# The Strassen stage of a hybrid decoder block: right-hand sums by accumulating transfers, no GpSimd sums, gates kept on chip

## The chip, the cores and the metric

The kernel runs on one core of one Trainium2 chip. The metric is the device time of one execution in microseconds (us), lower is better; it is given as the median of several runs. Five engines matter: TensorE (PE in the profile; its weight loads are PEld), VectorE (DVE), ScalarE (ACT), GpSimd (POOL) and SyncE (SP), which here only issues transfers. ACT and POOL issue transfers too. Each engine works through its own list of instructions in order.

## The reference, cut to what matters

One layer, 1024 tokens plus 16 meta tokens, width 1024, all in float32:

```python
xn = rms_norm(x, norm_pre)
proj = xn @ w_in                       # columns of four kinds, split:
y_ssd = ssd_mixer(z, xbc, dt, ...)     # Mamba-2 style chunked scan, ends in an rms_norm
y_sc  = short_conv_mixer(b, c, h, g)   # b * conv3(c * h) * silu(g)
y_dn  = gated_deltanet_mixer(qkv, z, b, a, ...)
branch = [y_ssd @ w_branch[0], y_sc @ w_branch[1], y_dn @ w_branch[2]]
gates  = sigmoid(gate_logits)          # 3 x 1024 columns of proj
merged = sum_n gates[n] * branch[n]
out = x + rms_norm(merged @ w_out, norm_post)
```

Seven products of 1024 x 1024 x 1024 stand at the end: three gates (`xn` with the last columns of `w_in`), three branches (`y` with `w_branch`), and the output (`merged` with `w_out`).

## The kernel before

**Precision.** Every float32 product is made of three TensorE products of numbers split in two: `a = ah + al`, and `ah*bh + ah*bl + al*bh`. ACT makes the high part with a copy that rounds, DVE the low part with a subtraction.

**The dense stage**, about 1300 us. The normalised input stands in SBUF, transposed, as `xh` and `xl` (pool `xp`). 84 jobs (`jobs`, `run_jobs`, `dense`) each load 128 columns of `w_in`, split them (L144 ACT, L145 DVE) and multiply them with the whole stream. Beside them run the mixers: `dn_mix` for 8 heads, `sd_mix` for 8 pairs of heads, `sc_jobs` for 8 blocks of channels. `weave` puts the mixers' small steps between the dense matmuls: a mixer is a generator that yields the amount of dense work wanted before its next step, scaled by `GAPS[kind]`. Mixers use POOL for masks (`affine_select`, L474, L568), for clearing buffers (L621) and for two subtractions near their end (L699, L703). Their results go to DRAM: `y_dn`, `y_sc`, `y_sd`, one [128, 1024] tensor for each of 8 row blocks. The stream is stored to `x_d` after the norm: ACT issues a store of `xh`, and POOL an accumulating transfer that adds `xl` to it in DRAM (L942, L943), 8 of each. Scratch tiles of mixers come from one tag of 5 buffers (`tmp`).

**The Strassen stage**, from L961 on. Each of the seven large products (a group: `ORDER_C` = gates 2, 1, 0, branches 2, 1, 0, output) is done with Strassen's method in the Winograd form: the operands are cut into 2 x 2 blocks of 512 x 512, and 7 products of blocks (phases `ph` 0 to 6) replace 8. A phase is 48 matmuls of 128x128 by 128x512: 4 quarters `q` of 12. The left operand (weights for TensorE) has blocks `a11` to `a22`, the right one (moving) `b11` to `b22`. Phases need these sums:

- right: `b11-b12`, `t2 = b22-b11`, `b12-b22`, `b21-t2`: POOL, 8 instructions a group in `sums_after` (L1047, L1082) and `t_prep` (L1058);
- left: `s2 = a22-a21` on DVE (L1068), and `a11-a21`, `a11+s2`, `a12-s2` on POOL through `both` (L1047), 6 instructions a group; the output group makes its `a11-a21` on DVE.

`t_prep` splits the right operand of the next phase (`th` ACT L1034, `tl` DVE L1035, two halves), `w_prep` the left one (`wh` ACT L1041, `wl` DVE L1042). The three matmuls are L1101 (`wh`,`th`), L1102 (`wh`,`tl`) and L1103 (`wl`,`th`). Results gather in two pairs of PSUM banks, `y` and `z`; `take_copy` (L1110, ACT) copies `y` after phases 0, 2 and 3, and `finish` (L1149, DVE) adds the copy to `z` for three of the four blocks of the result. For a gate group `block_done` applies the sigmoid and stores it to DRAM (`gate_d`, L1122, L1123); for a branch group it loads the gate again (L1116), multiplies (L1131) and adds to `merged` (L1133). The output group ends in `out_piece`. Right-hand blocks of gates and of two branches are loaded by rows, four transfers of 256 KB a block (L982); weights by one of 1 MB (L987). `scale_tasks` (L1196 on) loads `y_sd`, scales it by the norm (L1212) and stores it as `ys_d`.

The pools of the dense stage are closed before the Strassen stage; its pools `c1` and `c2` lie in the space that is freed, so the first tiles wait for the last readers of what lay there (`c1`'s first blocks lie where `xh` and `xl` lay).

**What sets the order.** The source gives each instruction a priority by its place; a list scheduler with a cost model then writes each engine's list ahead of time: an instruction that is not ready in the plan lets a later one pass. On the chip the lists are fixed.

## Time and profile before

| | |
|---|---|
| median of 3 runs | 1930.35 us (1929.93 to 1933.7) |
| profiled execution, its own time | 1933.35 us |
| its span, first to last instruction | 1931.6 us |
| PE busy | 1835.5 us, 95% of the span |
| DVE busy | 1380.2 us, 71% |
| ACT busy | 825.7 us, 43% |
| POOL busy | 474.2 us, 25% |
| mean granted TensorE clock | 0.982 of full |

A busy PE is not PE at its peak, since ends of matmuls are modelled; idle time of an engine is put down to what released it. The span is cut below at 1300.1 us, where the last dense matmul ends, and then at the first matmul of each group, which is seen in the change of the PSUM bank that the matmuls write.

### The profile page before, as it was taken

To read this page: it belongs to the slowest core of one execution; us is meant where nothing else is said; L and a number is where in the kernel's file an instruction comes from. 1 tells how busy PE (TensorE), PEld (TensorE's weight loads), DVE (VectorE), ACT (ScalarE), POOL (GpSimd) and SP (SyncE) were. 2 spreads that over 40 slices of the span, in tenths; PEclk is the share of its full clock that TensorE was granted. 3 is DMA by queue.
4 is the path that set the end of the run, shared out by engine and by line. 5 is a ranking of instruction groups with operands and counts; after the bars stand their busy time and mean duration, and the time that the engine had idled before them with its cause. 6 is when DMAs were issued, how large, how long until landed. Compare 5 with 4: busy or idle time off the path is not lost.

```text
span 1931.6 us, 27668 instructions
## 1 busy us (share of the span) xinstructions
PE 1835.5 (95%) x11115; PEld 1580.9 (82%) x11115; DVE 1380.2 (71%) x1842; ACT 825.7 (43%) x1341; POOL 474.2 (25%) x393
## 2 busy tenths in 40 slices
PE   6999999999999999999999999995999999998977
PEld 5988988898889888888898898884777787786856
DVE  5565666657666656765667887865786788989997
ACT  5533434243342523444254554623535444343434
POOL 3101011010100101110011111107273563829340
PEclk9999999999999999999999999997999999999989
DMA  6711112111111111111222231217817355261602
GB/s 183 197 33 56 45 45 66 34 45 55 45 55 55 34 56 44 55 50 40 59 77 64 80 107 56 77 39 260 308 73 236 117 188 170 92 229 49 202 22 87
DMA packets 143658, 182.77 MB, mean 95 GB/s; under 512 B 10689, under 2 KB 96894, under 8 KB 142506
## 3 DMA queue, kind: packets, MB, share of 16 engines
q1 hardware_dynamic: 135898, 153.22, 25.0%
q10 hardware_dynamic: 6336, 23.07, 3.0%
q0 software_dynamic: 1296, 4.72, 1.2%
q8 instruction: 87, 1.43, 0.3%
q14 instruction: 41, 0.34, 0.1%
HBM read 138.93 MB, written 42.05 MB: 94 GB/s over the span
## 4 chain that ended last, share of the span: by engine, by line
PE 75%; DVE 12%; issue 5%; DMA 3%; POOL 3%; ACT 2%; SPq 0%; DVEq 0%; ACTq 0%; POOLq 0%
DVE tl L1035 3%; PE py L1103 3%; PE py L1102 3%; DVE wl L1042 3%; PE py L1101 3%; PE pz L1103 2%; PE pz L1102 2%; PE pz L1101 2%; POOL t L1058 1%; DMA a__13894<-in_w_in_dram 1%; DVE s L1068 1%; DMA b__13498<-x_d 0%; DVE U L1149 0%; POOL b__16016 L1047 0%; DMA gain<-in_norm_pre_dram 0%
## 5 line engine op out<-in xcount | busy, mean ns | idle before, releaser
L1101 PE MATMUL py<-th,wh 128*128 128x512 f32 x448 | 179.2, 400 | 23.9 <-ACT wh L1041 20.5
L1103 PE MATMUL py<-th,wl 128*128 128x512 f32 x448 | 179.6, 401 | 17.8 <-DVE wl L1042 17.7
L1102 PE MATMUL py<-tl,wh 128*128 128x512 f32 x448 | 179.7, 401 | 12.5 <-DVE tl L1035 12.5
L1103 PE MATMUL pz<-th,wl 128*128 128x512 f32 x336 | 133.0, 396 | 8.1 <-DVE wl L1042 8.1
L144 ACT CAST wh<-raw 128x1024 fp32r<-128x1024 f32 x84 | 88.0, 1048 | 117.7 <-DMA raw<-in_w_in_dram 7.5
L1102 PE MATMUL pz<-tl,wh 128*128 128x512 f32 x336 | 132.6, 395 | 2.1 <-DVE tl L1035 2.1
L1101 PE MATMUL pz<-th,wh 128*128 128x512 f32 x336 | 132.5, 394 | 0.0
L145 DVE TENSOR_TENSOR wl<-raw,wh 128x1024 fp32r<-128x1024 f32 x84 | 103.4, 1230 | 34.3 <-ACT wh L144 34.3
L1101 PEld LDWEIGHTS py<-th,wh 128*128 128x128 f32 x448 | 86.8, 194 | 43.5 <-ACT wh L1041 21.3
L1103 PEld LDWEIGHTS py<-th,wl 128*128 128x128 f32 x448 | 86.8, 194 | 40.1 <-DVE wl L1042 22.1
L1102 PEld LDWEIGHTS py<-tl,wh 128*128 128x128 f32 x448 | 86.9, 194 | 33.2 <-DVE tl L1035 15.1
L1103 PEld LDWEIGHTS pz<-th,wl 128*128 128x128 f32 x336 | 64.2, 191 | 23.2 <-DVE wl L1042 9.9
L1102 PEld LDWEIGHTS pz<-tl,wh 128*128 128x128 f32 x336 | 64.1, 191 | 16.5 <-DVE tl L1035 3.0
L1101 PEld LDWEIGHTS pz<-th,wh 128*128 128x128 f32 x336 | 64.1, 191 | 13.3
L1035 DVE TENSOR_TENSOR tl<-t,th 128x1024 fp32r<-128x1024 f32 x14 | 43.2, 3083 | 13.8 <-ACT th L1034 13.8
L1042 DVE TENSOR_TENSOR wl<-s,wh 128x1024 fp32r<-128x1024 f32 x14 | 39.6, 2836 | 0.0
L1149 DVE TENSOR_TENSOR U<-pz,U 128x1024 f32<-128x1024 f32 x26 | 31.6, 1217 | 10.3 <-PE pz L1103 10.3
L1110 ACT COPY U<-py 128x1024 f32<-128x1024 f32 x28 | 28.2, 1007 | 6.9 <-DVE ys L1212 5.4
L1122 ACT ACTIVATE U<-U 128x1024 f32<-128x1024 f32 x12 | 12.7, 1062 | 42.7 <-DVE U L1149 42.7
L455 ACT ACT_TABLE_LOAD x20 | 25.7, 1283 | 4.3 <-PE sd6z L168 1.0
L1041 ACT CAST wh<-s 128x1024 fp32r<-128x1024 f32 x14 | 14.7, 1051 | 26.3 <-DVE s L1068 23.7
L1034 ACT CAST th<-t 128x1024 fp32r<-128x1024 f32 x14 | 14.7, 1051 | 25.3 <-POOL t L1058 18.3
(1899 smaller groups left out, 6065.2 us busy)
## 6 DMA issues: line engine op xcount, KB each, us to landing
raw<-in_w_in_dram SPq DMA_DIRECT2D x84, 512.0 KB, 4.1
g<-gate SPq DMA_DIRECT2D x24, 512.0 KB, 3.7
gate<-U ACTq DMA_DIRECT2D x12, 512.0 KB, 4.9
x_d<-xh ACTq DMA_DIRECT2D x8, 512.0 KB, 6.8
x_d<-xl POOLq DMA_DIRECT2D x8, 512.0 KB, 10.1
ys<-y_sd SPq DMA_DIRECT2D x16, 256.0 KB, 6.1
ys_d<-ys ACTq DMA_DIRECT2D x4, 1024.0 KB, 8.3
xt<-in_x_dram SPq DMA_DIRECT2D x7, 512.0 KB, 4.7
```

What stands on the lines that cost most here:

```text
L144: A.copy(wh, raws[i])
L145: V.tensor_tensor(wl, raws[i], wh.bitcast(F32), ALU.subtract)
L455: lambda o, c0, n: A.activation(dst[:, c0 - META:c0 - META + n], o, fn), name=name)
L1035: V.tensor_tensor(l, src, h.bitcast(F32), ALU.subtract)
L1042: V.tensor_tensor(l, src, h.bitcast(F32), ALU.subtract)
L1058: GP.tensor_tensor(t2, tk(k["b22"], u), tk(k["b11"], u), SUB)
L1068: V.tensor_tensor(wk(g.s2, u), wk(k["a22"], u), wk(k["a21"], u), SUB)
L1101: PE.matmul(o, lhsT=wh[:, k, cs], rhs=r1, start=fresh and k == 0, stop=False, skip_group_check=not fresh)
L1102: PE.matmul(o, lhsT=wh[:, k, cs], rhs=r2, start=False, stop=False, skip_group_check=not fresh)
L1103: PE.matmul(o, lhsT=wl[:, k, cs], rhs=r1, start=False, stop=k == HK - 1, skip_group_check=not fresh)
L1110: A.copy(t, g.ps["y", u])
L1149: V.tensor_tensor(t, z, t, ADD)
```

## The change

- **Right-hand operands** are kept in DRAM as seven ready blocks of 1 MB for each of five streams `s` (x, dn, sc, sd, wo): `opd[s][o]`, with off-diagonal blocks stored negated (`n12`, `n21`). The four sums are made by `sums(s)`: POOL issues four copies DRAM to DRAM and four accumulating transfers, each of which needs the one before. No POOL arithmetic is left in the Strassen stage. Phases 1, 4 and 5 (`NEG`) negate the left operand while it is split.
- **Where the sums run**: `right_x` and `right_wo` step along with `dn_mix` of heads 0 and 2, `sums("dn")` with `sd_mix` 1, one step after every third yield (`beside`); `sums("sc")` follows the last sc job, `sums("sd")` the scale tasks. The stores of the stream after the norm are gone; `right_x` makes them.
- **Left-hand sums** are all on DVE (`left_sum`).
- **Loads**: each phase loads its right operand as two transfers of 512 KB, two phases ahead (`t_load`, 4 buffers). The first two phases read `xh` and `xl` in SBUF, whose pool moved to the right side of SBUF and closes after them.
- **Order**: groups are gate 2, branch 2, gate 1, branch 1, gate 0, branch 0, output. A gate stays in four SBUF tiles until the next group uses it; `gate_d` is gone.
- **Passing**: after phase 0 (not in the first group) ACT copies bank `y` into bank `z`, where phases 1 to 2 go on adding, so that block (0,0) needs no addition on DVE.
- The scale tasks run one at every quarter from phase 2 of the first group, not one at every second quarter in groups 1 and 2. `GAPS["sl"]` is 2.6, not 3.6.

```diff
-GAPS = {..., "sl": 3.6}
+GAPS = {..., "sl": 2.6}
-    xp, xp_st = hand_pool("xp")
+    xp, xp_st = hand_pool("xp", side="right")
...
+    OPS = ("11", "n21", "t2", "t3", "t1", "t4", "22")
+    opd = {s: {o: dram.tile([P, HK, HALF], F32, name=f"{s}_{o}") for o in OPS + ("n12",)}
+           for s in ("x", "dn", "sc", "sd", "wo")}
...
+    def sums(s):
+        o = opd[s]
+        for dst, a, b in (("t1", "n12", "11"), ("t2", "t1", "22"), ("t3", "n12", "22"), ("t4", "t2", "n21")):
+            GP.dma_start(o[dst], o[a])
+            yield 0
+            GP.dma_start(o[dst], o[b], accum_op=ALU.add, max_dma_last_dim=2048)
+            yield 0
...
-        DMA.dma_start(y_dn[h], zT)
+        for j in range(2):
+            DMA.dma_start(quarter("dn", h // HK, j)[:, h % HK, :], zT[:, j * HALF:(j + 1) * HALF])
...
-            DMA.dma_start(y_sc[t], acc)
+            if t == KT - 1:
+                for _ in sums("sc"):
+                    pass
...
+    def right_x():
+        o = opd["x"]
+        for i in range(2):
+            ks, ts = slice(i * HK, (i + 1) * HK), slice(META + i * HALF, META + (i + 1) * HALF)
+            dst = quarter("x", i, i)
+            A.dma_start(dst, xh[:, ks, ts].bitcast(F32))
+            GP.dma_start(dst, xl[:, ks, ts].bitcast(F32), accum_op=ALU.add)
+        yield 0
+        for i in range(2):
+            ts = slice(META + (1 - i) * HALF, META + (2 - i) * HALF)
+            for u in range(2):
+                ks = slice(i * HK + 2 * u, i * HK + 2 * u + 2)
+                dst = quarter("x", i, 1 - i)[:, 2 * u:2 * u + 2, :]
+                for part in (xh, xl):
+                    t = tmp(f"xn{i}{u}")[:, :SEQ].rearrange("p (k t) -> p k t", k=2)
+                    A.mul(t, part[:, ks, ts].bitcast(F32), -1.0)
+                    if part is xh:
+                        A.dma_start(dst, t)
+                    else:
+                        GP.dma_start(dst, t, accum_op=ALU.add)
+                    yield 0
+        yield from sums("x")
...
+    def beside(main, side, every=3):
+        side = side()
+        for n, want in enumerate(main()):
+            yield want
+            if n % every == 0:
+                next(side, None)
+        for _ in side:
+            pass
...
-    for k in range(KT):
-        A.dma_start(x_d[k], xh[:, k, META:].bitcast(F32))
-        GP.dma_start(x_d[k], xl[:, k, META:].bitcast(F32), accum_op=ALU.add)
...
+    def t_load(g, ph):
+        if from_stream(g, ph):
+            return
+        for u in range(2):
+            t = g.raw[ph, u] = c1.tile([P, 2, HALF], F32, name=f"tr{g.n}_{ph}{u}", tag="tr", bufs=4)
+            DMA.dma_start(t, g.ops[OPS[ph]][:, 2 * u:2 * u + 2, :])
...
+        if ph in NEG and not from_stream(g, ph):
+            A.mul(w[:, 0], src, -1.0)
+            V.scalar_tensor_tensor(w[:, 1], src, -1.0, w[:, 0].bitcast(F32), ALU.mult, SUB)
...
+    def left_sum(g, dst, x, y, op):
+        k = g.blk
+        for u in range(2):
+            V.tensor_tensor(wk(k[dst], u), wk(k[x], u), wk(k[y], u), op)
...
+        if ph == 0 and g.n:
+            g.ps["z", u] = bank("z")
+            A.copy(g.ps["z", u], g.ps["y", u])
+        elif ph in (0, 2, 3):
+            t = g.st[ph, u] = c1.tile([P, 2, HALF], F32, tag=f"u{ph or 3}", name=f"u{ph}_{g.n}{u}", bufs=2)
             A.copy(t, g.ps["y", u])
...
+            gt, m = gate[i, j][:, qs, :], quarter_tile(merged, "mg", i, j)[:, qs, :]
+            if g.b == ORDER[0]:
+                V.tensor_tensor(m, t, gt, ALU.mult)
+            else:
+                V.tensor_tensor(gt, t, gt, ALU.mult)
+                V.tensor_tensor(m, m, gt, ADD)
...
+            if q == 1:
+                if ph == 3:
+                    left_sum(g, "a11", "a11", "s2", ADD)
                 elif ph == 4:
+                    left_sum(g, "a12", "a12", "s2", SUB)
+                elif ph == 6 and nxt is not None and nxt.kind != "o":
+                    left_sum(nxt, "a21", "a11", "a21", SUB)
...
+            if (0, 2) <= (g.n, ph) and extra:
+                extra.pop(0)()
```

## Rows read from the trace of the kernel before

**Rows 1.** engines over stretches: dense stage, then gap, seven groups, tail; busy us (count)

```profile
core 0: us, PE busy (x) PEld busy (x) DVE busy (x) ACT busy (x) POOL busy (x), PEclk, DMA share, GB/s
0.00:1300.10 1300.10, 1279.41 (x8763) 1130.39 (x8763) 861.50 (x1481) 549.53 (x1037) 165.32 (x297) 1.00 0.22 64
1300.10:1311.80 11.70, 0.01 (x1) 0.00 (x0) 3.14 (x3) 3.15 (x4) 0.00 (x0) 0.72 0.90 307
1311.80:1415.10 103.30, 84.07 (x337) 66.96 (x338) 72.88 (x56) 43.96 (x45) 57.15 (x20) 0.88 0.70 260
1415.10:1494.90 79.80, 76.72 (x337) 62.89 (x336) 61.83 (x36) 40.46 (x42) 42.32 (x15) 1.00 0.45 152
1494.90:1576.20 81.30, 77.08 (x337) 62.83 (x336) 64.45 (x37) 41.38 (x43) 43.15 (x15) 1.00 0.50 169
1576.20:1656.90 80.70, 78.14 (x337) 63.96 (x336) 70.33 (x44) 35.70 (x36) 42.83 (x14) 0.98 0.48 162
1656.90:1740.80 83.90, 79.73 (x337) 64.76 (x336) 77.15 (x51) 34.24 (x34) 43.41 (x14) 0.96 0.42 145
1740.80:1828.00 87.20, 79.23 (x338) 64.08 (x337) 82.35 (x51) 34.02 (x35) 50.89 (x14) 0.96 0.42 139
1828.00:1920.00 92.00, 80.54 (x336) 64.97 (x335) 78.42 (x73) 40.92 (x63) 29.12 (x10) 0.93 0.10 35
1920.00:1931.60 11.60, 0.52 (x3) 0.09 (x1) 8.16 (x18) 2.33 (x7) 0.00 (x0) 0.63 0.49 181
```

**Rows 2.** TensorE, order of time: first and last of the final phase's 48 matmuls

```profile
1909.47 0.39 PE L1101 MATMUL pz<-th,wh 128*128 128x512 f32 x1
...
1920.13 0.39 PE L1103 MATMUL pz<-th,wl 128*128 128x512 f32 x1
```

**Rows 3.** TensorE's waits, Strassen stage: total us, times, longest

```profile
PE py L1101 <- ACT wh L1041: 20.5, 2, 11.7
PE py L1103 <- DVE wl L1042: 17.7, 6, 8.7
PE py L1102 <- DVE tl L1035: 12.5, 6, 3.5
```

**Rows 4.** order of time, VectorE, then GpSimd, in the second group: start, us

```profile
1433.19 3.41 DVE L1042 TENSOR_TENSOR wl<-s,wh 128x1024 fp32r<-128x1024 f32 x1
...
1432.13 3.38 POOL L1047 TENSOR_TENSOR a__13971<-a__13971,s 128x1024 f32<-128x1024 f32 x1
```

**Rows 5.** VectorE's groups (busy us, mean ns); a scalar_tensor_tensor of 1024 (min/median/max)

```profile
L1149 DVE TENSOR_TENSOR U<-pz,U 128x1024 f32<-128x1024 f32 x26 | 31.6, 1217 | 10.3 <-PE pz L1103 10.3
...
L1035 DVE TENSOR_TENSOR tl<-b__16016,th 128x1024 fp32r<-128x1024 f32 x4 | 4.9, 1217 | 0.0
...
L444 DVE SCALAR_TENSOR_TENSOR dn2q<-dn2qraw,cols,dn2q x3: 1277/1280/1281, 288.8 to 292.6; 128x1024 f32<-128x1024 f32 x3
```

**Rows 6.** order of time around the gap: SP's weight load, ACT's rounding of it

```profile
1303.20 0.51 SPq L987 DMA_DIRECT2D a__13473<-in_w_in_dram  x1
...
1310.74 1.99 ACT L1041 CAST wh<-a__13473 128x1024 fp32r<-128x1024 f32 x2 [1.80 <-DMA a__13473<-in_w_in_dram]
```

**Rows 7.** VectorE, first group: in-order wait for a load

```profile
  DMA a__13894<-in_w_in_dram: 8.9, 1
```

**Rows 8.** GpSimd's accumulating stores L943 in the dense stage: issue ns, landing

```profile
L943 POOL DMA_DIRECT2D x_d<-xl x8: 840/848/1046, 45.9 to 70.2; - x8
...
  DMA x_d<-xh: 22.1, 8
...
DMA to landing us min/median/max: 5.7/10.1/13.0
```

**Rows 9.** transfers by issue: KB each, median us to landing

```profile
ys_d<-ys ACTq DMA_DIRECT2D x4, 1024.0 KB, 8.3
```

**Rows 10.** GpSimd, order of time at the start and in a mixer

```profile
4.56 0.37 POOL L621 MEMSET dm0Z<- 16x8 f16 x2
...
131.37 0.56 POOL L621 MEMSET dm0Z<- 128x256 f16 x2 [5.16 <-PE dm0u L633]
```

More of the change, by code (lines that the diff above doesn't have):

```diff
@@ L126, in hybrid_block @@
     snw = pers.tile([P, KT], F32, name="snw")
+    nsnw = pers.tile([P, KT], F32, name="nsnw")
     xh = xp.tile([P, KT, TK], F32R, name="xh")
@@ L240, in hybrid_block @@
     eps2 = cst.tile([P, 1], F32, name="eps2")
+    ndnw = cst.tile([P, 1], F32, name="ndnw")
     def constants():
@@ L915, in hybrid_block @@
             lambda t=t, g=g: sd_mix(t, grps[g], sdt[t])]
+        mix = lambda gens=gens: chain(*gens)
+        if t == 1:
+            mix = lambda mix=mix: beside(mix, lambda: sums("dn"))
         fs = []
@@ L989, in cols_of, with __init__ @@
         return load
-    def kept(blocks):
-        def load(t, i, j):
-            DMA.dma_start(t, blocks[i, j])
-        return load
-    ORDER_C = [("g", b) for b in ORDER] + [("b", b) for b in ORDER] + [("o", 0)]
-    right = {0: kept(ys_d), 1: rows_of(y_sc), 2: rows_of(y_dn)}
-    merged = {}
-    class Group:
-        def __init__(self, n, kind, b):
-            self.n, self.kind, self.b = n, kind, b
-            self.blk, self.t, self.w = {}, {}, {}
-            if kind == "g":
-                self.wsrc, self.tsrc = cols_of(w_in, C_G + b * D), rows_of(x_d)
-            elif kind == "b":
-                self.wsrc, self.tsrc = cols_of(w_branch[b]), right[b]
-            else:
-                self.wsrc, self.tsrc = None, cols_of(w_out)
+    groups = []
+    merged, gate = {}, {}
+    class Group:
+        def __init__(self, kind, b):
+            self.n, self.kind, self.b = len(groups), kind, b
+            self.blk, self.raw, self.t, self.w, self.ps, self.st = {}, {}, {}, {}, {}, {}
+            self.wsrc = {"g": cols_of(w_in, C_G + b * D), "b": cols_of(w_branch[b])}.get(kind)
+            self.ops = opd["x" if kind == "g" else "wo" if kind == "o" else ("sd", "sc", "dn")[b]]
         def load(self, *tags):
@@ L1025, in tk, with from_stream @@
-    def tk(t, u):
-        return t[:, 2 * u:2 * u + 2, :]
+    for b in ORDER:
+        for kind in "gb":
+            groups.append(Group(kind, b))
+    groups.append(Group("o", 0))
+    last = len(groups) - 1
     def wk(t, u):
         return t[:, :, u * 256:(u + 1) * 256]
-    def t_split(g, ph, u, src):
+    NEG = (1, 4, 5)
+    BANK = "yzyyzyz"
+    LEFT = ("a11", "a12", "s2", "a21", "a11", "a22", "a12")
+    def from_stream(g, ph):
+        return g.n == 0 and ph < 2
+    def t_load(g, ph):
[4 more added lines that the diff above has]
+            DMA.dma_start(t, g.ops[OPS[ph]][:, 2 * u:2 * u + 2, :])
@@ L1112, in gates_in @@
-    def gates_in(g, i, j):
-        if g.kind == "b":
-            for u in range(2):
-                t = g.gt[i, j, u] = slab(f"g{g.n}_{i}{j}{u}")
-                DMA.dma_start(t, gate_d[g.b, i, j, u])
-    def block_done(g, i, j, u, t, in_psum):
+            PE.matmul(o, lhsT=w[:, 0, k, cs], rhs=r1, start=fresh and k == 0, stop=False, skip_group_check=not fresh)
+            PE.matmul(o, lhsT=w[:, 0, k, cs], rhs=r2, start=False, stop=False, skip_group_check=not fresh)
+            PE.matmul(o, lhsT=w[:, 1, k, cs], rhs=r1, start=False, stop=k == HK - 1, skip_group_check=not fresh)
@@ L1124, in block_done @@
         elif g.kind == "b":
-            gt = g.gt.pop((i, j, u))
-            first = g.b == ORDER[0]
-            if first and (i, j) not in merged:
-                merged[i, j] = c2.tile([P, HK, HALF], F32, name=f"mg{i}{j}", tag=f"mg{i}{j}")
-            m = merged[i, j][:, 2 * u:2 * u + 2, :]
-            s = m if first else gt if in_psum else t
-            V.tensor_tensor(s, t, gt, ALU.mult)
-            if not first:
-                V.tensor_tensor(m, m, s, ADD)
-        else:
-            out_quarter(g, i, j, u, t, in_psum)
@@ L1188, in out_piece @@
             (DMA if jj else A).dma_start(out[t * P:(t + 1) * P, es], o)
-    def out_quarter(g, i, j, u, t, in_psum):
-        s = slab(f"o{i}{j}{u}") if in_psum else t
-        for v in range(2):
-            out_piece(g, i, j, u, v, t[:, v, :], s[:, v, :])
     def scale_tasks():
@@ new lines, in hybrid_block @@
+        if n + 2 < len(steps):
+            t_load(*steps[n + 2])
+        if nxt is not None:
+            nxt.load(*{3: ("a21",), 4: ("a11",), 5: ("a22",), 6: ("a12",)}.get(ph, ()))
+        if (g.n, ph) == (0, 2):
+            xp_st.close()
+            c2.append(ctx.enter_context(tc.tile_pool(name="c2", bufs=1, side="right", reuse_waits="tile")))
+        if g.kind == "o":
+            if ph == 0:
+                out_setup()
+            elif ph < 5:
+                residual(("a11", "a12", "a21", "a22")[ph - 1], 2 * (ph + 1) % 8)
```

272 lines of the change are left out of this document (116 added, 156 removed).

## The prediction

> **What bounds the kernel now.** Read the busy time by stretches first. In the dense stage TensorE is busy 1279.4 of 1300.1 us [rows 1], so nothing that other engines do faster there can show; only new waits can. In the seven groups of the Strassen stage TensorE has the same 336 matmuls each time, but the stretches are of 103.3, 79.8, 81.3, 80.7, 83.9, 87.2 and 92.0 us [rows 1]. What a group costs with no wait follows from the order of time: 48 matmuls start from 1909.47 to 1920.13, 47 steps of 0.2268 us [rows 2], so a phase is 10.9 us, a group 336 x 0.2268 = 76.2 us and seven groups 533.4 us. The groups lose 27.1, 3.6, 5.1, 4.5, 7.7, 11.0 and 15.8 us, 74.8 in all. Ahead of them lies a gap of 11.7 us, behind them a tail of 11.6 us. So 86.5 us ahead of the tail can be won and no more.
>
> What are they lost to? TensorE's waits name `wl`, `tl` and `wh`, operands that DVE and ACT split [rows 3]; one wait of 11.7 us is the gap itself. DVE is not full there: in the second group it is busy 61.8 of 79.8 us [rows 1]. But it is slow: a split of 128x1024 takes 3.41 us at 1433, while POOL runs a sum of 3.38 us [rows 4]. Four splits of another block take 1.217 us each, and the 26 additions that read one operand from PSUM keep a mean of 1.217 us through the whole stage [rows 5]. So an instruction of DVE with both operands in SBUF waits out POOL's sum, and late splits reach TensorE.
>
> **The change part by part.** *Sums leave POOL.* POOL's 308 us of sums in the stage [rows 1] end. The 40 left-hand ones go to DVE, 40 x 1.217 = 49 us; the 56 right-hand ones leave the engines. DVE's load in a branch group: 28 splits, 2 `s2` and 6 left sums, 36 x 1.217 = 43.8 us; 12 splits negate with scalar_tensor_tensor, 1.28 us each [rows 5], 0.8 us more; two blocks are added to what was kept, 4.9 us; 8 multiplications with gates and 8 additions, 19.5 us. That is 69 of 76.2 us; a gate group has 49.5. The load is not even: phases 5, 6 and 0 hold 12.2 us of DVE's work against 10.9, the next ones about 7 to 9.7. DVE falls 4 us behind and catches up, while splits are made a phase ahead. I take 2.5 us for each of three branch groups, 2 for the output group (its `a21` and `s2` follow the last block of `merged`) and 0.75 for each of two gate groups: 11 us for groups two to seven, against 47.7 now. Bounds: 3 (only a step or two short) and 30 (each branch group waits 8). ACT does the same splits, a copy from `y` to `z` in place of one to SBUF, and no more sigmoids than before: it was busy 34 to 44 us a group [rows 1], half of it.
>
> *The gap.* The first weights are issued at 1303.20, behind the right-hand blocks, and ACT rounds them at 1310.74 [rows 6]. In the changed kernel the right operand of two phases is in SBUF and the weight tile lies over the buffers of the dense stage's raw weights, which are read well before its end; so the load can go early and only PSUM is waited for, about 1 us. If the load goes only when the last dense matmul ends, 0.5 of issue, the 7 us from there to ACT's start and 1 us of rounding remain. I take 3 us, bounds 1 and 11.7.
>
> *First group.* Its 27.1 us were waits for loads and for POOL's sums behind them; DVE alone sat 8.9 us in front of a load [rows 7] with ready work behind it. Fewer loads are needed at once (two phases read SBUF), but the scale tasks and `sums("sc")` start here. I take 10 us, bounds 2 and 27.1.
>
> *Transfers.* A 1 MB store takes 8.3 us to land [rows 9]. Loads now have a phase or more of lead, 10.9 to 16 us. `sums("sc")` and `sums("sd")` run while POOL has nothing else to do and are wanted three and five groups later: nothing, if they leave loads enough room. Gates no longer go out and in, 24 MB less; right-hand loads grow by 19 MB.
>
> *The dense stage.* This is where the cost could come. POOL's list gets 22 transfers of `x` and `wo` beside two heads' mixers and 8 of `dn` beside `sd_mix`, each waiting for the one before. Behind such a wait stand the mixers' masks and clears, and behind them TensorE. Nearest rows: the accumulating stores of before take 0.85 us to issue, land in 10.1 us (least 5.7) for half a megabyte, and POOL sat 22.1 us in front of 8 of them, 2.8 each [rows 8]. Below, nothing: the list is planned, and POOL ran a mixer's clear at 4.56 us, ahead of work that stands earlier in the source [rows 10]; a transfer whose turn has not come lets later work pass, and only a landing later than planned blocks. Above, 30 x 2.8 = 84 us if every wait reached TensorE. A clear waits 5.16 us for TensorE's previous level [rows 10], so POOL has some slack. I take 4 us. ACT's 12 negations (1.0 us each, as its roundings [rows 6]) lie beside dense work; ACT is busy 549.5 of 1300 us. Scratch tiles: 8 more in a slot of 8 jobs, some 124 us (8 of 84 jobs in 1300 us), with 5 buffers, each held perhaps 20 us (estimated from two landings): enough. Dropping the `x_d` stores wins nothing: they were issued from 45.9 to 70.2 us [rows 8], and TensorE idles 21 us in the whole stage [rows 1]. `GAPS` 2.6 for the last mixer stays above the 2.4 of the other slots: nothing.
>
> The Trainium skill, "DMA: Bandwidth & Descriptors", section "Anatomy of one DMA — SWDGE (gpsimd) path", gives 2.0 us and bytes over 436 GB/s for a transfer issued by POOL, 3.2 us for half a megabyte; the row's least is 5.7 and its median 10.1, so the measured landing stands. By that rule the chains would be short and the 4 us would go to nothing, 1868.
>
> Sum: 1300.1 + 4 + 3 + 533.4 + 10 + 11 + 11.6 (tail, as it is) = 1873 us of span, 58 less. The profiled execution has 1.75 us around its span and lies 3.0 above the median of the runs, so the median is 1872 us.
>
> **The rivals.** *Transfers bind at the start.* In the first group the transfers already have a share of 0.70 at 260 GB/s [rows 1], some 370 GB/s when full. The changed group moves 13 MB of operands, up to 9 MB of scale tasks and 8 MB of sums in 80 us, as much as that holds. For it: DVE's 8.9 us. Against: the chain of sums is slow by itself and spreads. If the gap (11.7) and the first group (27.1) stay and two more groups lose 3 us each: 1872 + 8.7 + 17.1 + 6 = 1904. The Trainium skill, same page, section "Issuing engines are not separate DMA queues", says that transfers of all issuers run on the same 16 engines; that is this rival's mechanism, and no row here parts the issuers.
>
> *POOL's queue stalls the dense stage*, the other sign. Place: heads 0 and 2 and `sd_mix` 1. Price: at the bound of 2.8 us for each of 30, 84 instead of 4, 1952 us. It decides at 62 us, 2.1 us for each wait. For it: 2.8 is what a wait cost. Against: the planned order, the slack, and that nothing but transfers stood in POOL's way then. At half, it ends near 1910.
>
> *DVE becomes the bound* in branch groups: 8 us in each and in the output group instead of 2.5 and 2, 1872 + 22 = 1894. For it: 91% load, uneven; against: splits ahead by a phase.
>
> *DVE stays slow*, because POOL's issuing holds it as its sums did: half of the 36.7 us counted for groups two to seven stays away, and of the first group's 17.1 too, 1899. Against: 16 transfers of 0.85 us in the stage stand in place of 308 us.
>
> **How the numbers follow.** Forecast (1855 to 1890): 0.56. Better still, all terms at their low bounds (1300.1 + 0 + 1 + 533.4 + 2 + 3 + 11.6 - 1.3 = 1850): 0.08. Transfers bind: 0.15. DVE binds: 0.06. DVE stays slow: 0.02. POOL's queue: 0.13, of which 0.03 ends near 1910 and 0.10 above 1930. The range 1845 to 1912 holds the first five and the mild part of the last; beyond it I leave somewhat over 0.1. Within 0.2% (4 us, about what the runs can tell from none) 0.02; faster 0.88; slower 0.10.
>
> **What would show it.** No sum on POOL after 1300; DVE's splits at 1.2 to 1.3 us throughout; stretches of 76 to 80 us for groups two to seven, 86 for the first, a gap of about 3. TensorE's waits in the dense stage tell of POOL's queue: they should stay under 10 us, and POOL's waits for transfers should have no mixer's instruction behind them. I am wrong if the dense stage ends after 1320, or if the first group keeps waiting for `tr`, `a` or `ys` loads.

## The result and the profile after

The changed kernel takes 1903.37 us (median of 4 runs, 1900.59 to 1908.3), the kernel before took 1932.03 us beside it (4 runs): a ratio of 0.9854, 95% interval 0.9828 to 0.9879. It is faster by 28.7 us, a little under half of the 58 forecast. The time lies 31 us above the one forecast and outside the forecast's own band (1855 to 1890); it is inside the range only because that was drawn out to 1912 for the rivals. The profiled execution took 1900.59 us, its span 1898.3. The view by stretches, cut as in [rows 1] (dense stage, gap, seven groups, tail):

```profile
core 0: us, PE busy (x) PEld busy (x) DVE busy (x) ACT busy (x) POOL busy (x), PEclk, DMA share, GB/s
0.00:1324.35 1324.35, 1280.92 (x8763) 1132.09 (x8763) 859.23 (x1483) 566.01 (x1053) 179.86 (x323) 0.99 0.33 90
1324.35:1332.90 8.55, 0.01 (x1) 0.01 (x1) 0.72 (x2) 1.11 (x2) 2.08 (x2) 0.72 0.78 252
1332.90:1431.05 98.15, 86.26 (x336) 68.36 (x337) 62.73 (x62) 39.14 (x40) 4.64 (x7) 0.90 1.01 328
1431.05:1507.21 76.16, 76.16 (x337) 63.08 (x336) 57.22 (x51) 37.19 (x37) 3.07 (x4) 1.00 0.75 221
1507.21:1583.37 76.16, 76.16 (x337) 63.08 (x336) 48.33 (x42) 40.88 (x41) 0.00 (x0) 1.00 0.46 152
1583.37:1659.53 76.16, 76.16 (x337) 63.08 (x336) 58.71 (x51) 35.37 (x35) 0.00 (x0) 1.00 0.47 152
1659.53:1735.69 76.16, 76.16 (x337) 63.08 (x336) 53.07 (x47) 40.90 (x41) 0.00 (x0) 1.00 0.46 152
1735.69:1811.85 76.16, 76.16 (x337) 63.08 (x336) 56.26 (x49) 35.35 (x35) 0.00 (x0) 1.00 0.46 152
1811.85:1888.00 76.15, 76.15 (x337) 62.90 (x335) 60.11 (x73) 41.51 (x64) 0.00 (x0) 1.00 0.24 83
1888.00:1898.30 10.30, 0.17 (x1) 0.00 (x0) 7.24 (x15) 2.04 (x6) 0.00 (x0) 0.66 0.56 205
```

Groups two to seven are at the floor that was worked out from [rows 2]: TensorE is busy from first to last. VectorE's splits in the whole Strassen stage, answering to [rows 4, 5] (count, busy us, mean ns, idle before):

```profile
L1104 DVE TENSOR_TENSOR tl<-tr,th 128x1024 fp32r<-128x1024 f32 x94 | 114.1, 1222 | 67.4 <-ACT th L1103 66.8
L1164 DVE TENSOR_TENSOR u<-pz,u 128x1024 f32<-128x1024 f32 x29 | 35.4, 1219 | 7.6 <-PE pz L1141 7.6
```

No split waits out a sum any more. So groups two to seven did what the change is for, and more; the miss lies before the Strassen stage and at its head. Each term of the sum:

| term | forecast, us | after, us | off |
|---|---|---|---|
| dense stage ends at | 1304.1 | 1324.35 | +20.25 |
| gap | 3 | 8.55 | +5.55 |
| first group | 86.2 | 98.15 | +11.95 |
| groups two to seven | 468.2 | 456.95 | -11.25 |
| tail | 11.6 | 10.3 | -1.3 |

The terms add up to 25.2 us of span. The other 6 of the 31 us lie between span and median: the forecast put the median 1.3 us below the span of the profiled execution, and after it is 5.1 above.

Where the dense stage lost its 24 us against before is seen from the times at which TensorE starts its n-th matmul (difference to before in us, other columns: runs 1, 2, 10 and 12 below). The dense stage of runs 3 and 4 is that of the changed kernel and ended 1.8 us earlier, so 2 us of difference say nothing:

| n | before, at | after | run 1 | run 2 | run 10 | run 12 |
|---|---|---|---|---|---|---|
| 600 | 115.7 | +14.3 | +8.9 | +13.6 | -0.1 | -0.2 |
| 1000 | 166.0 | +22.9 | +19.2 | +13.6 | 0.0 | -0.1 |
| 2400 | 366.2 | +24.0 | +18.1 | +11.8 | +1.6 | +4.9 |
| 5000 | 729.5 | +23.5 | +18.1 | +10.6 | +7.8 | +3.1 |
| 7000 | 1020.1 | +23.0 | +18.0 | +9.8 | +7.5 | +3.5 |
| 8600 | 1268.6 | +23.5 | +18.0 | +9.9 | +10.7 | +3.5 |

14 us are lost by the 600th matmul, 9 more by the 1000th (in head 0's mixer, where the transfers of `x` stand), and little after. TensorE is idle for 43.4 us of the stage, 20.7 before. The rows of both places in the changed kernel; first ScalarE's queue, VectorE and TensorE at the start, in order of time (start, duration, what, idle before and its end):

```profile
0.81 0.68 ACTq L941 DMA_DIRECT2D wo<-in_w_out_dram  x1
1.57 0.59 ACTq L941 DMA_DIRECT2D wo<-in_w_out_dram  x1
...
15.80 0.29 DVE L343 TENSOR_SCALAR swb<-smw 128x256 fp32r<-128x256 f32 x1 [12.90 <-DMA smw<-in_w_in_dram]
...
17.84 4.07 PE L239 MATMUL xp<-ident,xg 128*128 128x128 f32 x20 [17.84 <-DVE xg L233]
...
45.27 0.55 PE L353 MATMUL sm<-xh,swa 128*64 128x346 f32 x1 [9.08 <-ACT xh L241]
```

and the window around that last wait:

```profile
40.00:50.00 10.00, 4.73 (x16) 3.58 (x17) 4.52 (x10) 4.74 (x11) 0.00 (x0) 0.50 0.34 134
```

The two 1 MB copies of `right_wo` (`wo_11`, `wo_22`) depend on nothing. The scheduler put them at the head of ScalarE's list, beside SyncE's first loads of `x` and of weights. VectorE stands 12.90 us in front of a split of `smw`, a small weight whose load lands at 15.8 us, and what the first transpose needs stands behind that split. TensorE starts at 17.8 us instead of 10.4 and waits 9.08 us more at 36.2; the window around that wait has a granted clock of 0.50, the lower level (1.2 GHz). Second, GpSimd in head 0's mixer and TensorE's wait for it:

```profile
156.36 1.03 POOL L126 DMA_DIRECT2D x_t<-x  x1 [2.43 <-DMA x_t<-x_t]
157.00 0.96 POOL L636 MEMSET dm0Z<- 128x256 f16 x2
168.40 0.53 POOL L124 DMA_DIRECT2D x_t<-x_t  x1 [10.44 <-DMA x_t<-x]
168.91 0.58 POOL L636 MEMSET dm0Z<- 128x256 f16 x2
...
169.31 0.29 PE L648 MATMUL dm0u<-dm0XU,dm0Z 128*128 128x64 f16 x4 [3.65 <-POOL dm0Z L636]
```

GpSimd sits 10.44 us in front of a transfer that waits for the landing of the one before; the mixer's clear behind it comes late, and TensorE waits 3.65 us. Between the 600th and the 1000th matmul TensorE is idle for 6.4 us, 4.6 of them before such clears; the rest of the 8.6 us passes while it is busy, with a granted clock of 0.86 from 150 to 160 us. In the first group VectorE waits for loads, each time with ready work behind (waits of one stretch: total us, times, longest):

```profile
DVE ys L1239 <- DMA ys<-y_sd: 13.4, 5, 4.7
...
DVE a__13694 L1126 <- DMA a__13776<-in_w_branch_dram: 7.4, 1, 7.4
DVE s L1112 <- DMA a__13462<-in_w_in_dram: 6.1, 1, 6.1
DVE a__13460 L1126 <- DMA a__13460<-in_w_in_dram: 5.6, 1, 5.6
```

TensorE itself waits 11.9 us in this group. The other 10.1 of its 22.0 us over the floor pass while it is busy (86.26 us for the work of 76.16), at a mean granted clock of 0.90. So both things that the prediction named as signs of being wrong are there: the dense stage ends after 1320, and the first group waits for `a` and `ys` loads.

### The profile page after: what moved, and what is told of

It reads as the page before. It is cut to its first block, busy times and chain, and to the rows that moved or that the text cites. A ratio compares the mean times of both kernels' runs of the same rounds, so it can differ in the third digit from the quotient of the medians.

```text
span 1898.3 us, 27585 instructions
## 1 busy us (share of the span) xinstructions
PE 1824.3 (96%) x11115; PEld 1578.8 (83%) x11115; DVE 1263.6 (67%) x1866; ACT 839.5 (44%) x1353; POOL 189.7 (10%) x335
## 3 DMA queue, kind: packets, MB, share of 16 engines
q1 hardware_dynamic: 135162, 162.65, 27.1%
q0 software_dynamic: 12976, 46.66, 10.6%
## 4 chain that ended last, share of the span: by engine, by line
PE 82%; DMA 7%; DVE 6%; issue 2%; ACT 1%; SPq 0%; POOL 0%; DVEq 0%; ACTq 0%; POOLq 0%
PE py L1141 5%; PE py L1140 5%; PE py L1139 5%; PE pz L1141 3%; PE pz L1140 3%; PE pz L1139 3%; DMA a__13462<-in_w_in_dram 1%; DMA ys<-y_sd 1%; DMA a__13776<-in_w_branch_dram 1%; DVE w L157 1%; DMA won<-in_w_out_dram 1%; DVE gt L1217 1%; DMA wo<-in_w_out_dram 1%; DMA xt<-in_x_dram 0%; DMA x_n<-xn 0%
## 5 line engine op out<-in xcount | busy, mean ns | idle before, releaser
L1141 PE MATMUL py<-th,w 128*128 128x512 f32 x432 | 170.1, 394 | 5.7 <-DVE w L1117 5.7
L1139 PE MATMUL py<-th,w 128*128 128x512 f32 x432 | 169.7, 393 | 1.7 <-ACT u L1151 1.7
L1140 PE MATMUL py<-tl,w 128*128 128x512 f32 x432 | 169.5, 392 | 1.9 <-DVE tl L1104 1.9
L1104 DVE TENSOR_TENSOR tl<-tr,th 128x1024 fp32r<-128x1024 f32 x94 | 114.1, 1222 | 67.4 <-ACT th L1103 66.8
L1103 ACT CAST th<-tr 128x1024 fp32r<-128x1024 f32 x94 | 98.4, 1052 | 106.0 <-PE py L1141 52.6
L1139 PE MATMUL pz<-th,w 128*128 128x512 f32 x320 | 124.5, 389 | 0.0
L1140 PE MATMUL pz<-tl,w 128*128 128x512 f32 x320 | 124.5, 389 | 0.0
L1141 PE MATMUL pz<-th,w 128*128 128x512 f32 x320 | 124.5, 389 | 0.0
L157 DVE TENSOR_TENSOR w<-raw,w 128x1024 fp32r<-128x1024 f32 x84 | 103.5, 1232 | 10.5 <-ACT w L156 9.8
L1141 PEld LDWEIGHTS py<-th,w 128*128 128x128 f32 x432 | 82.1, 190 | 23.5 <-DVE w L1117 6.5
L156 ACT CAST w<-raw 128x1024 fp32r<-128x1024 f32 x84 | 88.0, 1048 | 23.1 <-PE sc2h L180 4.0
L1139 PEld LDWEIGHTS py<-th,w 128*128 128x128 f32 x432 | 82.1, 190 | 19.2 <-ACT u L1151 2.1
L1139 PEld LDWEIGHTS pz<-th,w 128*128 128x128 f32 x320 | 60.1, 188 | 12.4
L1141 PEld LDWEIGHTS pz<-th,w 128*128 128x128 f32 x320 | 60.1, 188 | 12.4
L239 PE MATMUL xp<-ident,xg 128*128 128x128 f32 (+1 forms) x72 | 11.0, 304 | 21.2 <-DVE xg L233 20.8
```

What stands on the lines that cost most here:

```text
L156: A.copy(wh, raws[i])
L157: V.tensor_tensor(wl, raws[i], wh.bitcast(F32), ALU.subtract)
L239: PE.transpose(pv[:, k, :], xg[:n, kk * P:(kk + 1) * P], ident[:n, :n])
L1103: A.copy(h, src)
L1104: V.tensor_tensor(l, src, h.bitcast(F32), SUB)
L1139: PE.matmul(o, lhsT=w[:, 0, k, cs], rhs=r1, start=fresh and k == 0, stop=False, skip_group_check=not fresh)
```

## The experiments

Each is the changed kernel with the edit shown, unless it says otherwise.

**1. The copies of w_out held back.**

```diff
-                A.mul(t, t, -1.0)
+                held = A.mul(t, t, -1.0)
...
-            A.dma_start(quarter("wo", i, i), w_out[...])
+            with tc.issue_after(held.ins):
+                A.dma_start(quarter("wo", i, i), w_out[...])
```

> The changed kernel with one edit: the two 1 MB copies of w_out into wo_11 and wo_22, which depend on nothing and stood at the head of ScalarE's queue at 0.8 and 1.6 us, are queued behind the multiply that is written ahead of them. Theory A (these copies took the transfers that the first weights and rows of x waited for): the first transpose is back from 17.8 us to about 10.4, the 200th matmul comes 14 to 15 us earlier, the dense stage ends near 1310 instead of 1324.4, and the time is about 1888 us (1903 - 15). Rival (the late start comes from the other order of SyncE's loads, weights ahead of rows of x, or from the pool on the other side): the first transpose stays near 17.8 and the time near 1903. If the order of the loads carries a part of it, something between, 1892 to 1898.

1890.4 us (5 runs), 0.9776 of before (0.9763 to 0.979): 13 us less. The first transpose is back at 10.48 us, but the dense stage ends only 5.5 us earlier, at 1318.84: a second loss had been hidden behind the first. GpSimd, then TensorE, in this run:

```profile
46.77 1.24 POOL L913 DMA_DIRECT2D x<-xl  x1 [31.65 <-DMA x<-xh]
47.48 0.75 POOL L280 MEMSET rows<- 128x128 f32 x1
...
56.97 0.45 PE L289 MATMUL pr<-ident,rows 128*128 128x128 f32 x1 [7.16 <-DMA rows<-in_dn_norm_dram]
```

The clear of `rows` stands behind an accumulating store of `right_x` that waits for the store before it; the loads into `rows` wait for the clear, and TensorE 7.16 us for them. Theory A holds for the first transpose, and a different part of the change takes over half of what it gives. But the edit takes back two things and doesn't part them. Without the early copies the plan is another one too: in this run, as before, VectorE's split of `smw` stands behind the first steps of the norm (it runs at 13.05 us, the first step at 7.07), and SyncE's first loads have the order of before. (The two profiled spans differ by 7.3 us only: that of the changed kernel was its fastest run, this one the slowest of its five.)

**2. No sums in the dense stage.**

```diff
-        yield from sums("x")
...
-        yield from sums("wo")
...
-            mix = lambda mix=mix: beside(mix, lambda: sums("dn"))
...
+        return [o[k] for k in ("11", "n21", "n12", "11", "n12", "n21", "22")]
```

> The changed kernel without the sums of x, of w_out and of dn in the dense stage (12 plain and 12 accumulating transfers of 1 MB each on GpSimd's queue); the Strassen stage reads quarters in their place, so its loads are as many and as large. The copies of w_out at the start and the sign changes stay. The sums of x, w_out and dn are thus left out of the output. Theory B (GpSimd's own work of dm0 and dm2 stands in its queue behind transfers that wait for transfers): the 8.4 us that the dense stage loses between the 600th and the 1000th matmul, and the 3 us near the 2400th, go, so the dense stage ends near 1313 to 1315 and the time is about 1893 us. Rival (these gaps come from the multiplies by -1 on ScalarE and their stores, which stay): time within 2 us of 1903.

1888.8 us, 0.9765 (0.9752 to 0.9779). Between the 600th and the 1000th matmul the loss is 0.0 us instead of 8.6, and the dense stage ends at 1310.85, 13.5 earlier. Theory B holds, with more than it claimed; the multiplies by -1, which stay, cost nothing that shows there.

**3. No scale tasks.**

```diff
-    extra = scale_tasks()
+    extra = []
...
-            ... ("sd", "sc", "dn")[b]]
+            ... ("sc", "sc", "dn")[b]]
```

> The changed kernel without the scale tasks of the first Strassen group (16 loads of 256 KB, 16 multiplies on VectorE, 4 stores of 1 MB and the eight transfers of the sums of sd); branch 0 then reads the operands of branch 1, so the output lacks branch 0. Theory C (the first group loses its later half to these loads and multiplies, which stand in SyncE's, VectorE's and ScalarE's order): gaps of 1.7, 1.9, 1.8 and 3.9 us from 1378 on go, with the low clock after them, and the first group takes about 86 to 88 us instead of 98.2, the time is about 1892. Rival (the whole loss comes from the burst of weight blocks and operands before 1365, and what is lost later is that backlog): first group 95 or more, time 1900 or more.

1885.6 us, 0.9752 (0.9739 to 0.9765). The first group:

```profile
1331.03:1415.30 84.27, 81.32 (x336) 65.89 (x337) 54.69 (x48) 41.65 (x42) 1.53 (x2) 0.94 0.75 234
```

Theory C holds: 13.9 of its 22 us over the floor were the scale tasks, that is these loads and multiplies with their stores and the sums of sd.

**4. No sums of sc either**, beside the edit of 3.

```diff
-            if t == KT - 1:
-                for _ in sums("sc"):
-                    pass
...
+            ... ("dn", "dn", "dn")[b]]
```

> The changed kernel without the scale tasks of the first group (as the run that left them out) and also without the eight transfers of the sums of sc, four of which run from 1328 to 1365; branches 0 and 1 then read the operands of branch 2, so the output lacks both. With the scale tasks alone left out the first group took 84.3 us from its first matmul to that of the second, 8.1 over 76.2, with a gap of 2.9 us on a weight split and the low clock at its head. Theory (the sums of sc and the 3 MB of weight blocks share the transfers there): the 2.9 us gap goes or falls below 1 and the first group takes 79 to 82, time 1881 to 1883 us. Rival (the weight blocks are late only because they are issued late): first group 84 again, time within 1.5 us of 1885.6.

1881.0 us, 0.9725 (0.971 to 0.9741). The first group:

```profile
1330.60:1410.50 79.90, 79.84 (x337) 65.01 (x338) 55.24 (x48) 41.92 (x42) 0.00 (x0) 0.96 0.55 196
```

The wait of 2.9 us is gone. These transfers and the weight blocks do slow one another: the fourth block, issued at 1327.6 in run 3 and 1327.5 here, lands after 24.2 us there and after 10.7 here. The 3.7 us that stay over the floor are the lower clock (0.96): TensorE is idle for less than 0.1 us.

**5. Only the first weight block earlier.**

```diff
-                DMA.dma_start(quarter("sc", t // HK, j)[:, t % HK, :], s)
+                (GP if t == KT - 1 else DMA).dma_start(quarter("sc", t // HK, j)[:, t % HK, :], s)
```

> The changed kernel with the last two stores of the sc branch on GpSimd's queue instead of SyncE's, so that the load of the first weight block a11 no longer stands behind a store that waits for the last dense result. Theory D (the load was late only because of its place in SyncE's queue): a11 is issued before 1320, and the gap from the last dense matmul to the first of the Strassen stage shrinks from 8.5 to 2 to 4 us, so about 1898 us. Rival (the room for a11 comes free only when the last dense weights are used): a11 is issued at 1324 or later, gap 7 to 9 us, time 1903.

1901.4 us, 0.9832 (0.9819 to 0.9846): nothing gained. SyncE's queue and TensorE in order of time, then the gap and the first group by windows:

```profile
1310.67 0.39 SPq L1047 DMA_DIRECT2D a__13450<-in_w_in_dram  x1
1324.78 0.39 SPq L1047 DMA_DIRECT2D a__13458<-in_w_in_dram  x1
...
1351.01 0.80 PE L1141 MATMUL pz<-xh,w 128*128 128x512 f32 x1 [10.96 <-DVE w L1120]
```

```profile
1321.13:1322.00 0.87, 0.00 (x0) 0.03 (x1) 0.83 (x2) 0.00 (x0) 0.00 (x0) 1.00 0.00 0
1322.00:1430.32 108.32, 85.22 (x337) 67.80 (x338) 64.52 (x63) 40.26 (x41) 8.88 (x11) 0.87 0.96 317
```

Theory D is right about the gap (0.87 us), which is given back in the group: the second block is issued at 1324.78, 3.7 us behind the last dense matmul and so as late as before (3.9), and TensorE waits 10.96 us for its split. At the head of this stage several loads are late, and one alone mended moves the wait.

**6. GpSimd's sums put back, spread.** Two useless sums per product in groups 3 to 7.

```diff
+        if g.n > 1:
+            GP.tensor_tensor(fin["pj"], src, src, SUB)
...
```

> The changed kernel with 14 useless GpSimd subtractions of 128x1024 put into each of the groups 3 to 7 (two per product, reading the operand that VectorE splits at that time, writing a tile that nobody reads): about the number that each group had before. Theory (the prediction's: VectorE's 3.41 us splits and the groups of 80 to 92 us of before came from GpSimd's sums beside them): VectorE's 128x1024 splits and sums in those groups go from 1.22 us to a mean of 2 us or more, those groups grow from 76.2 to 79 to 92 us, and the time to 1918 to 1947 us. Rival (the groups were long before because of the order of loads and splits, and VectorE's slowness alone is covered): the splits slow down, but the groups stay within 1 us of 76.2 and the time within 5 us of 1903.

1914.8 us, 0.9899 (0.9885 to 0.9913): 11 us more, below the theory's range. VectorE is slow again (its `tl` splits have a mean of 1532 ns, its busy time in these groups goes from 276.5 to 362.3 us), but the groups grow only from 380.8 to 392.4 us, where the kernel before took 425.1:

```profile
1509.87:1902.26 392.39, 383.31 (x1681) 314.59 (x1679) 362.34 (x263) 193.34 (x216) 173.94 (x66) 1.00 0.39 135
```

So a slow VectorE alone was not all of it; runs 7 to 9 ask what else.

**7. The kernel before without GpSimd's sums.**

```diff
+        if eng is GP:
+            return
...
-            GP.tensor_tensor(t2, tk(k["b22"], u), tk(k["b11"], u), SUB)
-            t_split(g, ph, u, t2)
+            t_split(g, ph, u, tk(k["b22"], u))
```

> The kernel before without GpSimd's 14 sums in each Strassen group: the splits read the unsummed blocks, so the output lacks these sums; loads, gate stores, the order of the groups and all of VectorE's and ScalarE's work stay. Groups 3 to 7 took 425.1 us in the kernel before (76.2 each would be 380.8). Theory (the excess of the groups in the kernel before came from GpSimd's sums, by contention or by standing in the chain): groups 3 to 7 take 381 to 388 us together and the time falls by 40 us or more, to 1895 or less. Rival (it came from the order of the groups, the gates through DRAM and the reloads): groups 3 to 7 take 405 us or more, time above 1912.

1863.0 us, 0.9632 (0.9619 to 0.9646). First group, then groups 3 to 7:

```profile
1311.52:1392.91 81.39, 78.97 (x336) 64.42 (x337) 55.81 (x56) 44.10 (x45) 0.00 (x0) 0.97 0.91 333
1469.08:1849.90 380.82, 380.82 (x1681) 315.13 (x1679) 268.78 (x250) 187.14 (x208) 0.00 (x0) 1.00 0.41 141
```

All that groups two to seven lost came from GpSimd's sums (the second takes 76.17 too, from 1392.91 to 1469.08), and 21.9 of the first group's 27.1 us. The order of the groups, the gates through DRAM and the reloads, all still there, cost nothing that shows.

**8. The kernel before with the sums written aside.**

```diff
+            if eng is GP:
+                d = c2.tile([P, 2, HALF], F32, name="aside", tag="t2", bufs=2)...
+            eng.tensor_tensor(d, fn(x, u), fn(y, u), op)
...
-            t_split(g, ph, u, t2)
+            t_split(g, ph, u, tk(k["b22"], u))
...
```

> The kernel before with GpSimd's 14 sums in each Strassen group made, but written aside to a tile that nobody reads; the splits read the unsummed blocks (the output lacks the sums). So VectorE has GpSimd beside it as before, but no split waits for a sum. In the changed kernel 14 such sums put back cost groups 3 to 7 only 11.5 us (392.3 instead of 380.8), where the kernel before lost 44.3 in them. Theory (the larger part of the loss was the wait for sums that themselves took 3.4 to 10 us beside VectorE, the smaller the slower splits): groups 3 to 7 take 388 to 400 us. Rival (the slower VectorE alone made the loss, and the changed kernel bears it better by its order): groups 3 to 7 stay above 412 us.

1939.2 us, 1.0029 (1.002 to 1.0039). Groups 3 to 7 take 428.1 us, as slow as before, although no split waits for a sum:

```profile
1495.88:1924.00 428.12, 395.56 (x1681) 321.35 (x1679) 371.50 (x254) 187.49 (x210) 194.88 (x61) 0.96 0.37 127
```

My theory fell: being in the chain was not what cost. In the second last group ten sums stand in one row; GpSimd, then VectorE:

```profile
1733.19 6.33 POOL L1062 TENSOR_TENSOR t<-b__16230,b__16074 128x1024 f32<-128x1024 f32 x2 [9.42 <-DMA b__16230<-ys_d]
1739.48 6.66 POOL L1051 TENSOR_TENSOR aside<-b__16230,b__15998 128x1024 f32<-128x1024 f32 x2
1746.10 6.63 POOL L1051 TENSOR_TENSOR aside<-b__16152,b__16074 128x1024 f32<-128x1024 f32 x2
1752.70 6.77 POOL L1051 TENSOR_TENSOR aside<-a__16076,s 128x1024 f32<-128x1024 f32 x2
1759.43 6.68 POOL L1051 TENSOR_TENSOR aside<-a__16232,s 128x1024 f32<-128x1024 f32 x2
...
1747.14 3.35 DVE L1042 TENSOR_TENSOR wl<-a__16076,wh 128x1024 fp32r<-128x1024 f32 x1
1750.42 1.21 DVE L1134 TENSOR_TENSOR g<-py,g 128x1024 f32<-128x1024 f32 x1
```

For these 33 us VectorE's instructions on two SBUF operands take 3.4 us each (one with an operand in PSUM 1.21), and TensorE waits 8.4 and 5.1 us. In the kernel before there are rows of twelve (from 1566.6 us on, for 38.2 us). In run 6 the sums stand mostly in pairs. Hence the new theory: it is the length of the row.

**9. As 6, but ten in a row, then four.**

```diff
+        if g.n > 1 and u == 0 and ph in (3, 6):
+            GP.tensor_tensor(fin["pj"], src, src, SUB)
+            for _ in range(9 if ph == 3 else 3):
+                GP.tensor_tensor(fin["pj"], fin["pj"], fin["pk"], SUB)
```

> The changed kernel with the same number of useless GpSimd sums in groups 3 to 7 as in the run that put 14 back (there two per product, groups 3 to 7 took 392.3 us), but ten of them in one row in the middle of each group and four in a row near its end, as they stood in the kernel before and in the run that wrote them aside (ten in a row over 33 us there, and groups 3 to 7 of 428.1 us). Theory (what counts is how many sums stand in one row: VectorE then runs at 3.4 us a piece for some 30 us, longer than its lead over TensorE lasts): groups 3 to 7 take 405 to 428 us, and the time is 1928 to 1950 us. Rival (the order of the changed kernel bears the slow VectorE wherever it falls): groups 3 to 7 take 385 to 398 us and the time stays at 1908 to 1920 us.

1961.0 us, 1.0136 (1.0119 to 1.0153), and groups 3 to 7 take 438.1 us: the theory's direction, but both beyond its ranges. Groups 3 to 7 as one window, then GpSimd, VectorE and TensorE in one row of ten:

```profile
1512.92:1951.06 438.14, 395.10 (x1681) 321.46 (x1679) 402.33 (x257) 192.52 (x216) 216.64 (x70) 0.95 0.35 120
```

```profile
1691.47 29.71 POOL L1108 TENSOR_TENSOR pj<-pj,pk 128x1024 f32<-128x1024 f32 x9
...
1702.33 3.41 DVE L1104 TENSOR_TENSOR tl<-tr,th 128x1024 fp32r<-128x1024 f32 x1
...
1715.67 0.79 PE L1145 MATMUL py<-th,w 128*128 128x512 f32 x1 [9.32 <-DVE w L1124]
```

Seventy sums cost 57.3 us in rows and 11.6 us in pairs. A split is made about a product ahead, and a row of 30 us uses that lead up; between single sums VectorE, which has some 100 us of idle time in these groups, can catch up. The two runs differ in one more thing. The sums here read two tiles, those of 6 one tile twice: VectorE's instructions take 3.4 us beside the former and 2.9 beside the latter. And VectorE's busy time here, 402.3 us, is itself more than the floor of 380.8, so some 21 of the 57 us may be plain load. Run 8 has rows of two-tile sums with 371.5 us of VectorE's time, less than the floor, and loses 47.3 us; so the rows cost much by themselves. No run has two-tile sums in pairs, which would part the two shares.

**10. Only the dense stage mended**, all work done: the edit of 1, and

```diff
-        GP.memset(rows1, 0.0)
+        V.memset(rows1, 0.0)
...
-            GP.dma_start(o[dst], o[a])
+            tc.keep_in_program_order(GP.dma_start(o[dst], o[a]))
...
+            if n in (2, 7, 12, 36, 44, 52):
+                next(side, None)
...
-        if h in (0, 2):
-            mix = lambda mix=mix, side=(right_x, right_wo)[h // 2]: beside(mix, side)
+        mix = lambda mix=mix: spread(mix, dense_side)
```

> The changed kernel with all its work, and only the dense stage's order mended: the two copies of w_out queued behind a late multiply; the second tile of convolution weights cleared by VectorE instead of GpSimd (so that it doesn't stand behind a transfer that waits for a transfer); the transfers of x and w_out spread over the first six dn mixes at places where GpSimd's other work isn't due, each kept in the order in which it is written. Theory (all of the +24 us of the dense stage is the early copies and GpSimd's queue): the dense stage ends at 1300 to 1306 instead of 1324.4, the Strassen stage stays as it was (gap 8.5, first group 98), time about 1880 us. Rival (multiplies by -1, the extra stores and the 20 more MB slow the dense stage wherever they stand): the dense stage ends at 1312 or later, time 1890 or more.

1885.0 us, 0.9749 (0.9736 to 0.9761). The dense stage ends at 1311.55. The start is whole (-0.1 us at the 600th matmul, 0.0 at the 1000th), but later the stage loses again, 10.7 us by the 8600th (table above), by the transfers at their new places as I read it; run 12 bears on that. Neither theory is quite right: spreading does not make them free.

**11. The head of the Strassen stage mended too**, all work done: the edits of 10 and 5; the tiles `w`, `tr` and `gpost` in a pool `c0` ahead of the weight blocks; the loads of the scale tasks on GpSimd's queue, well ahead of their multiplies; the sums of sc behind them.

```diff
+    c0 = ctx.enter_context(tc.tile_pool(name="c0", bufs=1, reuse_waits="tile"))
...
-            if t == KT - 1:
-                for _ in sums("sc"):
-                    pass
...
-                    DMA.dma_start(box[i, j][:, k, :], y_sd[...])
+                GP.dma_start(box[i, j][:, k, :], y_sd[...])
...
+            for s in ("sc", "sd"):
+                for _ in sums(s):
+                    pass
```

> The run with the mended dense stage, and the head of the Strassen stage mended too: the last two sc stores on GpSimd's queue; the tiles w, tr and gpost in a pool of their own ahead of the weight blocks, so that all four blocks can be loaded before the last dense weights are free; the loads of the scale tasks on GpSimd's queue, ahead of their multiplies by several products; the sums of sc moved behind them. All work is done. Theory (the excess of the first group and the gap come from the order of these loads): gap 1 to 4 us, first group 78 to 88, time about 1855 to 1865 us. Rival (given back later, as in the run that only issued a11 early: there the gap fell from 8.5 to 0.9 and the first group grew from 98.2 to 108.3): first group 95 or more, time 1870 or more.

1865.9 us, 0.9649 (0.9636 to 0.9662). Gap 0.87 us, first group 86.04: this time nothing is given back. Several edits were made at once, and no run parts them.

**12. GpSimd's transfers thinned out**, all work done: the sums of w_out in the Strassen stage behind those of sc and sd, those of dn one transfer at the end of each sd mixer.

```diff
-            if n in (2, 7, 12, 36, 44, 52):
+            if n in (2, 9, 40, 48):
...
-        yield from sums("wo")
...
-            for s in ("sc", "sd"):
+            for s in ("sc", "sd", "wo"):
...
+    dn_side = sums("dn")
+
+    def aside(main):
+        yield from main()
+        next(dn_side, None)
```

> The run with both stages mended (1865.9 us, dense stage to 1313.9), with GpSimd's transfers of the dense stage thinned out further: the sums of x alone in the dn mixes, the sums of dn one transfer in each of the eight sd mixes, the sums of w_out in the Strassen stage behind those of sc and sd. All work is done. Theory (the dense stage's remaining +13 us are GpSimd's transfers that stand ahead of its other work while they wait for the one before): the dense stage ends at 1300 to 1306, and the time is 1852 to 1860 us. Rival (the sums cost it by their traffic wherever they stand): dense end 1311 or later, time 1864 or more.

1857.5 us (5 runs), 0.9608 (0.9595 to 0.9621). Dense stage, gap, first group, groups two to seven:

```profile
0.00:1304.30 1304.30, 1281.07 (x8763) 1130.85 (x8763) 860.11 (x1484) 568.22 (x1055) 173.41 (x311) 1.00 0.30 84
1304.30:1305.17 0.87, 0.00 (x0) 0.03 (x1) 0.84 (x2) 0.84 (x1) 0.00 (x0) 1.00 1.02 403
1305.17:1388.15 82.98, 79.57 (x337) 64.02 (x337) 60.94 (x60) 38.97 (x40) 13.79 (x24) 0.98 0.90 311
1388.15:1845.13 456.98, 456.98 (x2017) 378.36 (x2015) 335.17 (x309) 231.27 (x253) 14.79 (x19) 1.00 0.61 191
```

The best version is 45.9 us below the changed kernel and does all its work. It lies 5.4 us below run 7, which leaves the sums out.

## Why the prediction was right in sign and wrong in size

*Sums leave POOL*: right. 69.6 of the 74.8 us that the groups lost came from those sums (run 7). The 11 us allowed for VectorE's uneven load were not needed: VectorE was busy for 56 to 59 us of a branch group, not 69, and six groups lose nothing. The explanation in the first part was short of one thing: what made the slow VectorE cost so much was not only that each split waits out a sum, but that up to twelve sums stood in a row (run 6 against 8 and 9, with the share of the second tile open). The Trainium skill, "SBUF — State Buffer", section "SBUF: two separate sides", says that an instruction of VectorE with two SBUF inputs and a GpSimd instruction that reads SBUF share one pair of ports, that whichever starts first has it for its whole length, and that the other fully blocks. The rows agree: 3.41 us beside a sum [rows 4], 1.21 with one operand in PSUM beside a sum (run 8).

*The dense stage*, "I take 4 us": the step that failed, and most of the miss (+20.25 us). It had two faults. There was no term for the transfers of `right_wo` on ScalarE's queue, although the same part says, of a clear, that the planner lets early-ready work go ahead of what stands earlier in the source: a copy of a kernel input from DRAM to DRAM is ready from the start, and the plan put it there. Run 1 shows this at the first transpose; the copies and the clear behind the accumulating store cover one another, so that 8.9 of the 14 us stay when the first alone is mended, and none when both are (run 10). And GpSimd's queue was priced at a slack that the clears do not have: 8.6 us in head 0 alone, 13.5 for all sums of the dense stage (run 2): a sixth of the rival's 84, but three times the 4. The waits themselves were longer than 2.8 us each: GpSimd sat 107 us in front of the transfers of `x`, `wo` and `dn` in the dense stage (without the first store of `x`, 41.1), where 30 x 2.8 makes 84, and up to 12.9 us in front of one. The Trainium skill's rule, "DMA: Bandwidth & Descriptors", section "Anatomy of one DMA — SWDGE (gpsimd) path", makes an estimated 4.4 us for 1 MB (2.0 us and bytes over 436 GB/s); the accumulating copies of 1 MB here took 8.1 to 21.2 us to land. The measurement decides.

*The gap*, 3 us against 8.55: the prediction's own late case, 0.5 and 7 and 1 us, was right to 0.1; the choice of 3 was not. "The load can go early" did not look at SyncE's list, where the load stands behind the last store of sc, which waits for the last dense result. Run 5 shows that place to be the cause, and that mending it alone is worth nothing.

*The first group*, 10 us over the floor against 22.0: mis-sized. 13.9 us are the scale tasks (run 3), 4.4 the sums of sc (run 4), and the remaining 3.7 the lower clock. In the changed kernel 10.1 of the 22.0 us pass at that lower clock, for which the prediction had no term. The rival "transfers bind at the start" gave 1904 us, close to the result, but by luck: it has a kept gap of 11.7, a first group 27.1 over the floor and two more slow groups; the later groups lost nothing, and the dense stage made up the number. Its mechanism is real in this group alone. "DVE becomes the bound" and "DVE stays slow" did not happen.

What stays open: how much of run 2's gain is waiting and how much traffic. Spreading (run 10) left 11.5 us at the end of the dense stage, and thinning (run 12), which also took the eight transfers of `wo` out of it, 4.2; that speaks for waiting at the place of issue, but no run issues the same transfers from a queue that nobody else needs. Open too is how much of the late start is the copies' traffic and how much the order that was planned around them.

## What to carry to other kernels

Work that depends on nothing was put first by the list scheduler: before adding a transfer ask what it is ready for, and tie it to a late instruction if it is not wanted early. A transfer that waits for another transfer blocks all that stands behind it in its engine's list, so chains of them belong where that engine has nothing else to do, one link at a time. GpSimd's sums beside a busy VectorE were dearest in rows; if they can't go, spread them; and when a load at the head of a stage is mended, look which load is late next before counting the gain.
